# One SBUF room for h2 of all dense tokens from the second merge on, and the dots of two first keys at that merge's end

## Chip, core and metric

The kernel runs on one core of one Trainium2 chip. The metric is the device time of one execution in microseconds. Before the change it is 3731.83 us, the median of three runs (3722.95 to 3736.19).

## What is computed

One decoder block over 1024 tokens of width 1024: an RWKV-7 time mixing and a sparse attention side by side, a merge of both with a layer norm, and PEER, a product-key retrieval of single-neuron experts. The change touches the merge of the second half of the tokens and the beginning of PEER:

```python
merged = sigmoid(z_ga) * y_a + sigmoid(z_gb) * y_b
x  = layer_norm(ALPHA * x + gt1 * (merged @ w_out))
h2 = x * (1 + sc2) + sh2
# _peer(h2): 8 heads, 128 x 128 keys, the best 16 of each half
q = (ht @ w_pq).reshape(T, 8, 2, 64)
s = einsum('thcd,hcnd->thcn', q, sub_keys)
s1, i1 = top_k(s[:, :, 0], 16);  s2, i2 = top_k(s[:, :, 1], 16)
top_s, pos = top_k(s1[..., :, None] + s2[..., None, :], 16)
experts = i1 * 128 + i2 (at pos);  gates = softmax(top_s)
act = gelu(einsum('cd,chkd->chk', h, u_tab[experts])) * gates
out = einsum('chk,chkd->cd', act, v_tab[experts])
```

## The kernel before

Tokens are worked on in two halves H of 512. For each half the program computes both branches, the projection of the attention branch (`merge_b`) and then `merge(H)`. PEER follows. Of its 1024 tokens the first `TD` = 384 (tiles 0 to 2) have their experts' rows gathered from DRAM; the other `DN` = 640 (tiles 3 to 7; a tile has 128 tokens) are done densely: for each of the 128 first keys i1 the dots of all 640 tokens with the 128 experts of that key, times a table of gates that is zero where an expert wasn't chosen, and then the second table.

All float32 products are made of two parts, hi and lo (`whi`, `wlo` for weights): ACT copies the raw weight to `whi`, POOL subtracts it from the raw one to give `wlo`, and PE runs hi by hi, hi by lo and lo by hi. `copy` (L233) is ACT's copy; where a line reads L233, the names on it tell which step it is.

`merge(1)` works in this order: the split of the RWKV output into `ya`; `wbra` (L424 to L426 on PE, sums `zs` L1023 and L1024 on DVE, split into `big`); `wout` (sum `vt` L1043 on DVE); the layer norm with its transposes; h2 with its split into `h2T`; then `wq` in eight heads, whose result goes to the DRAM tensor `qTD`. `ya` and then `h2T` lie in one tile, `Q`, of 128 x 2 x 8 x 512 numbers (hi and lo). After the split, two POOL DMAs store `h2T` to the DRAM tensor `h2TD` (merge 0 stores its 128 dense tokens there too). Beside the merge, a generator `side` retrieves the experts of tiles 1 to 3 on DVE; a step of it (one of four for a tile) is four score tables `sc` (transposing matmuls L1134 on PE from `qT`, a load of `qTD`; copies on ACT), and on DVE four MAX8 (L1143), four MATCH_REPLACE8 (L1145), four MAX8 (L1147) and eight FIND_INDEX8 (L1149, L1151).

Then `retr1` begins. Eight POOL DMAs read `h2TD` back into a new tile `h2T` of 128 x 2 x 8 x 640 (L1633). From it `dots_ahead` takes the dots of 69 first keys, ahead of the dense stage: for one key SP loads `raw` (L1273), ACT makes `whi`, POOL `wlo` (L1277), PE runs 48 matmuls of 128x320 in 24 pairs (L1290, L1292, L1294), ACT copies the result to `ds` and SP stores it to `dotD`. Three keys stand first; after that, in `beside`, steps of the retrieval of tiles 4 to 7 (DVE), batches of the gate tables of tiles 3 to 7, gathers for tiles 0 to 2 (POOL, DVE) and two keys of dots take turns. A tile's gate table can begin when its slots are there (transposes L1239 on PE, waiting for DVE's L1199); a batch of it is 8 copies `gt` and 2 copies `st` on ACT and transposes L1264 on PE. What is left of tables and dots is done at the end of `retr1`. The dense stage follows, in which PE runs the other dots and the second table for all 128 keys.

The order of the instructions on each engine is set by the scheduler of the tile framework, which plays the program through a timeline of its own and puts on each queue what it finds ready first; each engine works through its queue in that order.

Of the kernel before, what the change touches and what calls it, by code (L numbers as in the profile page):

```python
# [8 lines left out]
F32 = mybir.dt.float32  # L9
F32R = mybir.dt.float32r  # L10
# [14 lines left out]
RB = 2  # L25
WB = 3
# [9 lines left out]
REUSE = "tile"  # L36
# [7 lines left out]
QIB = 2  # L44
GM = 1
# [7 lines left out]
DN = 1024 - TD  # L53
# [150 lines left out]
def body(tc, a, out, dbg=None, ntiles=8, mark=lambda s: None):  # L204
# [16 lines left out]
    def prw():  # L221
        return banks[0].tile([128, 512], F32, name="rw", bufs=4)
# [782 lines left out]
    def merge(H, y, bz, mp, side, ties):  # L1005
        t0 = H * 512
        big = lambda name: (bz if name == "big" else mp).tile([128, 2, 8, 512], F32R, name=name)
# [52 lines left out]
        for tt in range(4):  # L1060
            pl = [pacc(), pacc()] if tt == PA else [prw(), prw()]
            for d in range(8):
                nc.tensor.transpose(pl[d // 4][:, d % 4 * 128:(d % 4 + 1) * 128], vt[:, d, tt * 128:tt * 128 + 128], ident)
            xn = mp.tile([128, 1024], F32, name="xn", bufs=4)
            xns.append(xn)
            layernorm(xn, pl, mp)
            for n in range(2):
                pl = ptp()
                for d in range(4):
                    nc.tensor.transpose(pl[:, d * 128:(d + 1) * 128], xn[:, (4 * n + d) * 128:(4 * n + d + 1) * 128], ident)  # L1070
                copy(hl[:, 4 * n:4 * n + 4, tt * 128:tt * 128 + 128], pl.rearrange("p (a b) -> p a b", a=4))
# [9 lines left out]
        if c0 < 512:  # L1081
            for n in range(2):
                G.dma_start(h2TD[:, n, :, dst], h2T[:, n, :, c0:])
# [14 lines left out]
        for h in range(8):  # L1098
# [9 lines left out]
            if H:  # L1108
                next(side, None)

# [371 lines left out]
    h2TD = tc.dram_tile([128, 2, 8, DN], F32R, name="h2TD")  # L1482
# [15 lines left out]
    for H in range(2):  # L1498
# [109 lines left out]
        if H == 1:  # L1608
            tkp = tc.tile_pool(reuse_waits=REUSE, name="tk", bufs=1, side="right")
            tk = tkp.__enter__()  # L1610
        with tc.tile_pool(reuse_waits=REUSE, name=f"mg{H}", bufs=1) as mp:
# [6 lines left out]
            merge(H, ys[4 * H + 3], big, mp, side, ties if H == 0 else iter(()))  # L1618
# [7 lines left out]
    with tc.tile_pool(reuse_waits=REUSE, name="du", bufs=1) as du, \  # L1626
            tc.tile_pool(reuse_waits=REUSE, name="pg", bufs=1, space=PSUM) as pg:

        for name, bufs in (("raw", RB), ("whi", WB), ("wlo", WB)):
            du.tile([128, 1024], F32 if name == "raw" else F32R, name=name, bufs=bufs)  # L1630
        h2T = du.tile([128, 2, 8, DN], F32R, name="h2T")
        for k in range(8):
            G.dma_start(h2T[:, :, k], h2TD[:, :, k])  # L1633
        act = {}
        mark("retr1")
        with tc.tile_pool(reuse_waits=REUSE, name="slots", bufs=1) as sl, \
# [18 lines left out]
            def dots_ahead():  # L1655
                for i1 in ahead:
# [97 lines left out]
```

## Time and profile before

| | |
|---|---|
| median of three runs | 3731.83 us |
| the profiled execution | 3729.43 us |
| its span in the trace | 3727.7 us |
| PE, DVE, ACT, POOL busy | 94%, 69%, 45%, 53% of the span |
| `merge(1)` | about 1488 to 1651 us |
| `retr1` | about 1651 to 2351 us |
| dense stage | about 2351 to 3727 us |

Times within a trace count from the start of the span. PE's busy share is that of pipelined matmuls and says little alone; the stretches below, the waits and the timelines of single engines say which engine sets the pace in a stage. A row of a timeline reads: start, duration, engine, line, operation, what it writes and reads, shape, count, and in brackets how long the engine had been idle and whose end released it. Rows of several instructions alike are put together as x2 and so on.

### The profile page before, as it was taken

The page shows a single profiled execution, that of the slowest core. Times are in us where ns is not written, and L with a number is a line of the kernel's source. Part 1 is how long each engine was busy: PE and PEld are TensorE (multiplying, and loading weights), DVE is VectorE, ACT ScalarE, POOL GpSimd, SP SyncE. Part 2 cuts the span into 40 slices and gives each one's busy share as a digit, 9 for nine tenths or more (in the row PEclk, how much of TensorE's full clock was granted, in tenths as well). Part 3 has the DMA queues.
Part 4 walks back from the last instruction along what each step waited for, and adds up shares of the span by engine and source line. Part 5 has one row for each costly group of instructions (what it writes and reads, how often), then busy time and mean ns, then how long its engine had stood idle before and what let it go on. Part 6 is the DMA issues. An engine that isn't in the chain of part 4 may idle for free.

```text
span 3727.7 us, 64789 instructions
## 1 busy us (share of the span) xinstructions
PE 3499.9 (94%) x24045; PEld 3135.1 (84%) x24045; DVE 2587.5 (69%) x5433; ACT 1694.3 (45%) x3230; POOL 1987.4 (53%) x1572
## 2 busy tenths in 40 slices
PE   8999999889999989879999999999999999999997
PEld 7677777666677767669999999999999999999987
DVE  7856653847467764899989985467667776677654
ACT  3649953244344443447676688422222322222223
POOL 5442222354455554336656542467677676777655
PEclk9999999989999999989999999999999999999999
DMA  7453323864667666478888874889989999898873
GB/s 232 151 159 104 107 87 124 291 194 163 215 206 224 213 213 207 135 230 319 318 327 316 316 284 151 300 320 324 339 317 331 332 330 338 320 332 325 306 263 120
DMA packets 436880, 920.95 MB, mean 247 GB/s; under 512 B 36452, under 2 KB 195508, under 8 KB 433876
## 3 DMA queue, kind: packets, MB, share of 16 engines
q1 hardware_dynamic: 311956, 498.38, 39.8%
q0 software_dynamic: 124608, 418.43, 31.5%
q8 instruction: 189, 3.10, 0.3%
q14 instruction: 127, 1.04, 0.1%
HBM read 791.59 MB, written 125.08 MB: 246 GB/s over the span
## 4 chain that ended last, share of the span: by engine, by line
PE 51%; DVE 15%; DMA 12%; ACT 7%; issue 6%; POOL 6%; SPq 0%; POOLq 0%; ACTq 0%; DVEq 0%
PE pair L1294 8%; PE pair L1292 8%; PE pair L1290 8%; PE acc L424 4%; PE acc L425 4%; PE acc L426 4%; DMA g<-in_u_dram,gidx 4%; DMA g<-in_v_dram,gidx 3%; ACT gt L233 3%; POOL g L1391 2%; DMA raw<-in_ut_dram 2%; POOL wlo L1277 2%; DVE g L1395 2%; PE tp L1264 2%; PE acc L976 1%
## 5 line engine op out<-in xcount | busy, mean ns | idle before, releaser
L1277 POOL TENSOR_TENSOR wlo<-raw,whi 128x1024 fp32r<-128x1024 f32 x264 | 648.7, 2459 | 378.2 <-ACT whi L233 354.5
L414 POOL TENSOR_TENSOR wlo<-wraw,whi 128x512 fp32r<-128x512 f32 x280 | 371.1, 1328 | 550.7 <-ACT whi L233 497.2
L233 ACT ACTIVATE whi<-raw 128x1024 fp32r<-128x1024 f32 x264 | 278.9, 1057 | 649.4 <-PE pair L1292 382.9
L1391 POOL DMA_INDIRECT g<-in_u_dram,gidx x361 | 376.6, 1043 | 293.7 <-DVE g L1395 187.6
L1399 DVE SCALAR_TENSOR_TENSOR pg<-g,dots,pg 128x1024 f32<-128x1024 f32 x317 | 407.0, 1284 | 146.0 <-DMA g<-in_v_dram,gidx 143.0
L1290 PE MATMUL pair<-A,whi 128*128 128x320 f32 (+2 forms) x2048 | 480.5, 311 | 25.4 <-DVE A L1322 19.4
L1290 PE MATMUL pair<-h2T,whi 128*128 128x320 f32 x2048 | 475.6, 312 | 15.0 <-ACT whi L233 15.0
L1292 PE MATMUL pair<-A,whi 128*128 128x320 f32 (+2 forms) x2048 | 479.9, 311 | 3.8 <-DVE A L1322 3.6
L1294 PE MATMUL pair<-A,wlo 128*128 128x320 f32 (+2 forms) x2048 | 478.7, 310 | 0.8 <-POOL wlo L1277 0.8
L1292 PE MATMUL pair<-h2T,whi 128*128 128x320 f32 x2048 | 474.7, 311 | 0.0
L1294 PE MATMUL pair<-h2T,wlo 128*128 128x320 f32 x2048 | 473.1, 311 | 1.6 <-POOL wlo L1277 1.6
L1391 POOL DMA_INDIRECT g<-in_v_dram,gidx x320 | 311.7, 974 | 187.4 <-DVE pg L1399 90.7
L424 PE MATMUL acc<-big,whi 128*128 128x512 f32 x864 | 356.6, 414 | 23.1 <-DVE zs L532 6.5
L1290 PEld LDWEIGHTS pair<-A,whi 128*128 128x128 f32 x2048 | 347.4, 189 | 28.0 <-issue 19.9
L1290 PEld LDWEIGHTS pair<-h2T,whi 128*128 128x128 f32 x2048 | 343.9, 188 | 16.9 <-ACT whi L233 15.4
L426 PE MATMUL acc<-big,wlo 128*128 128x512 f32 x864 | 351.8, 408 | 1.7 <-POOL wlo L414 1.7
L425 PE MATMUL acc<-big,whi 128*128 128x512 f32 x864 | 349.9, 405 | 2.4 <-DVE big L450 2.3
L1292 PEld LDWEIGHTS pair<-A,whi 128*128 128x128 f32 x2048 | 347.4, 189 | 5.1 <-DVE A L1322 5.1
L1395 DVE SCALAR_TENSOR_TENSOR g<-g,pg 128x1024 f32<-128x1024 f32 x233 | 281.3, 1216 | 101.3 <-DMA g<-in_u_dram,gidx 100.2
L1294 PEld LDWEIGHTS pair<-A,wlo 128*128 128x128 f32 x2048 | 347.5, 189 | 1.0 <-POOL wlo L1277 1.0
L1294 PEld LDWEIGHTS pair<-h2T,wlo 128*128 128x128 f32 x2048 | 342.9, 188 | 3.4 <-POOL wlo L1277 2.4
L1292 PEld LDWEIGHTS pair<-h2T,whi 128*128 128x128 f32 x2048 | 344.1, 188 | 0.6
(482 smaller groups left out, 6673.1 us busy)
## 6 DMA issues: line engine op xcount, KB each, us to landing
raw<-in_vt_dram SPq DMA_DIRECT2D x136, 512.0 KB, 4.2
raw<-in_ut_dram SPq DMA_DIRECT2D x128, 512.0 KB, 5.5
gtD<-st SPq DMA_DIRECT2D x20, 2048.0 KB, 9.8
gt<-gtD SPq DMA_DIRECT2D x32, 1280.0 KB, 14.5
wraw<-in_wz_dram SPq DMA_DIRECT2D x152, 256.0 KB, 3.2
dotD<-ds SPq DMA_DIRECT2D x69, 320.0 KB, 5.7
al<-dotD SPq DMA_DIRECT2D x69, 320.0 KB, 6.5
mw<-in_wada_dram SPq DMA_DIRECT2D x32, 512.0 KB, 5.4
```

What stands on the lines that cost most here:

```text
L233: copy = lambda o, i, **k: A.activation(o, i, AF.Copy, **k)
L414: G.tensor_tensor(lo, raw, hi.bitcast(F32), op=OP.subtract)
L424: mm(pt, lhsT=wh[:, ks], rhs=ah[:, k, :], start=k == 0, stop=False)
L425: mm(pt, lhsT=wh[:, ks], rhs=al[:, k, :], start=False, stop=False)
L426: ins = mm(pt, lhsT=wl[:, ks], rhs=ah[:, k, :], start=False, stop=k == nk - 1)
L1277: G.tensor_tensor(lo, raw, hi.bitcast(F32), op=OP.subtract)
L1290: mm(pts[n], lhsT=wh, rhs=ah[:, h], start=k == 0, stop=False)
L1292: mm(pts[n], lhsT=wh, rhs=al[:, h], start=False, stop=False)
L1294: latest[:] = [mm(pts[n], lhsT=wl, rhs=ah[:, h], start=False, stop=last)]
L1391: G.indirect_dma_start(out=u, out_offset=None, in_=a["u" if n < 2 else "v"], in_offset=bass.IndirectOffsetOnAxis(ap=idx[:, k:k + 1], axis=0))
L1395: V.scalar_tensor_tensor(u, u, 1.0, h2, op0=OP.mult, op1=OP.mult, accum_out=dots[:, k:k + 1])
L1399: V.scalar_tensor_tensor(acc, u, dots[:, k:k + 1], acc, op0=OP.mult, op1=OP.add)
```

## The change

- A tile `h2A` (named `h2T`) of 128 x 2 x 8 x 640 numbers is made before the second merge, on the right side of SBUF, and lives until the end. In the second merge `Q` is no tile of its own but the last 512 of the 640 columns of `h2A`. The 128 dense tokens of the first merge, which are all that is still stored to `h2TD`, are loaded into the first 128 columns at the start of the second merge (two POOL DMAs). The two stores of the second merge and the eight loads at the beginning of `retr1` are gone.
- In the second merge `xn` has two buffers, not four.
- At the end of the second merge, behind `wq`, the dots of the first two keys of `ahead` are taken (48 matmuls each, into the PSUM tiles `rw`), with weights that go through the merge's `wraw`, `whi`, `wlo` in halves; ACT copies each result in two pieces to `zs` and itself issues the two stores to `dotD`. `dots_ahead` begins with the third key, so 67 are left to it.
- The pools of `retr1` are laid out in another order (`gt`, `wlo`, `raw`, `whi`).

```diff
--- before.py
+++ after.py
@@ -42,6 +42,7 @@
 SQ = 6
 XOB = 2
 QIB = 2
+DOTS0 = 2
 GM = 1
 FIRST = 3
 XR = 3
@@ -1002,9 +1003,18 @@
         for _ in rest:
             pass
 
-    def merge(H, y, bz, mp, side, ties):
+    def merge(H, y, bz, mp, side, ties, h2A=None):
+
         t0 = H * 512
-        big = lambda name: (bz if name == "big" else mp).tile([128, 2, 8, 512], F32R, name=name)
+
+        def big(name):
+            if name == "Q" and h2A is not None:
+                return h2A[:, :, :, DN - 512:]
+            return (bz if name == "big" else mp).tile([128, 2, 8, 512], F32R, name=name)
+
+        if h2A is not None:
+            for n in range(2):
+                G.dma_start(h2A[:, n, :, 0:DN - 512], h2TD[:, n])
         ya = big("Q")
         for k in range(4):
             st = stg.tile([128, 512], F32, name="xt")
@@ -1061,7 +1071,7 @@
             pl = [pacc(), pacc()] if tt == PA else [prw(), prw()]
             for d in range(8):
                 nc.tensor.transpose(pl[d // 4][:, d % 4 * 128:(d % 4 + 1) * 128], vt[:, d, tt * 128:tt * 128 + 128], ident)
-            xn = mp.tile([128, 1024], F32, name="xn", bufs=4)
+            xn = mp.tile([128, 1024], F32, name="xn", bufs=2 if H else 4)
             xns.append(xn)
             layernorm(xn, pl, mp)
             for n in range(2):
@@ -1078,9 +1088,9 @@
             if "h2" in dbg:
                 nc.sync.dma_start(dbg["h2"][d * 128:(d + 1) * 128, t0:t0 + 512], h2)
             split_act(h2T[:, 0, d, :], h2T[:, 1, d, :], h2)
-        if c0 < 512:
+        if c0 < 512 and not H:
             for n in range(2):
-                G.dma_start(h2TD[:, n, :, dst], h2T[:, n, :, c0:])
+                G.dma_start(h2TD[:, n], h2T[:, n, :, c0:])
         for tt, xn in enumerate(xns[:max(0, NG - 4 * H)]):
 
             i = H * 4 + tt
@@ -1107,6 +1117,19 @@
             nc.sync.dma_start(qTD[H][:, h, :], qt)
             if H:
                 next(side, None)
+        for i1 in list(ahead)[:DOTS0] if H else ():
+
+            w = split_w(a["ut"][i1], 1024)
+            pts = [prw()[:, 0:DN // 2] for n in range(2)]
+            for k in range(8):
+                wh, wl = w[k // 4]
+                ks = slice(k % 4 * 128, k % 4 * 128 + 128)
+                mm6(pts, wh[:, ks], wl[:, ks], h2A[:, 0, k, :], h2A[:, 1, k, :], k, k == 7)
+            for n in range(2):
+                zs = stg.tile([128, 512], F32, name="zs")[:, 0:DN // 2]
+                copy(zs, pts[n])
+                A.dma_start(dotD[ahead[i1]][:, n * (DN // 2):(n + 1) * (DN // 2)], zs)
+            next(side, None)
 
     def layernorm(dst, src, mp):
 
@@ -1479,7 +1502,7 @@
             early_found[i] = f
 
     qTD = [tc.dram_tile([128, 8, 512], F32, name=f"qTD{i}") for i in range(2)]
-    h2TD = tc.dram_tile([128, 2, 8, DN], F32R, name="h2TD")
+    h2TD = tc.dram_tile([128, 2, 8, DN - 512], F32R, name="h2TD")
     gtD = tc.dram_tile([DN // 32, 128, 128, 32], F32, name="gtD")
     ahead = [i1 for i1 in range(128) if i1 % 8 < (J0 + (i1 // 8 % 16 < EXTRA) if i1 >= 8 else JF)]
     ahead = {i1: n for n, i1 in enumerate(ahead)}
@@ -1606,6 +1629,8 @@
             nc.sync.dma_start(dbg["ya"][:, :, H * 512:H * 512 + 512], yaD[H])
             nc.sync.dma_start(dbg["yb"][:, :, H * 512:H * 512 + 512], ybD[H])
         if H == 1:
+            hp = es.enter_context(tc.tile_pool(reuse_waits=REUSE, name="h2", bufs=1, side="right"))
+            h2A = hp.tile([128, 2, 8, DN], F32R, name="h2T")
             tkp = tc.tile_pool(reuse_waits=REUSE, name="tk", bufs=1, side="right")
             tk = tkp.__enter__()
         with tc.tile_pool(reuse_waits=REUSE, name=f"mg{H}", bufs=1) as mp:
@@ -1615,7 +1640,7 @@
 
                 side = retrieve_all(range(1, M1), tk, keep)
             mark(f"merge{H}")
-            merge(H, ys[4 * H + 3], big, mp, side, ties if H == 0 else iter(()))
+            merge(H, ys[4 * H + 3], big, mp, side, *((ties,) if H == 0 else (iter(()), h2A)))
             for _ in side:
                 pass
         bz.close()
@@ -1626,11 +1651,10 @@
     with tc.tile_pool(reuse_waits=REUSE, name="du", bufs=1) as du, \
             tc.tile_pool(reuse_waits=REUSE, name="pg", bufs=1, space=PSUM) as pg:
 
-        for name, bufs in (("raw", RB), ("whi", WB), ("wlo", WB)):
+        du.tile([128, 20, 128], F32, name="gt", bufs=2)
+        for name, bufs in (("wlo", WB), ("raw", RB), ("whi", WB)):
             du.tile([128, 1024], F32 if name == "raw" else F32R, name=name, bufs=bufs)
-        h2T = du.tile([128, 2, 8, DN], F32R, name="h2T")
-        for k in range(8):
-            G.dma_start(h2T[:, :, k], h2TD[:, :, k])
+        h2T = h2A
         act = {}
         mark("retr1")
         with tc.tile_pool(reuse_waits=REUSE, name="slots", bufs=1) as sl, \
@@ -1653,7 +1677,7 @@
 
 
             def dots_ahead():
-                for i1 in ahead:
+                for i1 in list(ahead)[DOTS0:]:
                     ds = sl.tile([128, DN], F32, name="ds", bufs=4)
                     copy(by_half(ds), dots_u(i1, du, h2T, 2))
                     nc.sync.dma_start(dotD[ahead[i1]], ds)
```

Nearly every queue has another order from the second merge on. On DVE, at the end of the second `merge_b` (its last sums are L999 before, L1000 after; `zs` L1023 before and L1033 after are the first sums of the merge; MAX, MATCH_REPLACE and MAX_INDEX are retrieval steps), before:

```order
L999 SCALAR_TENSOR_TENSOR zs<-zs,acc 128x512
L450 TENSOR_TENSOR Q<-xt,Q 128x384 x2
L999 SCALAR_TENSOR_TENSOR zs<-zs,acc 128x512 x2
L1023 SCALAR_TENSOR_TENSOR zs<-zs,acc 128x512
L1143 MAX v_14009<-sc 128x8
L1024 TENSOR_TENSOR zs<-zs,xt 128x512
L1143 MAX v_14009<-sc 128x8 x3
L1145 MATCH_REPLACE s_14022<-v_14009,sc 128x128
L1149 MAX_INDEX i_14010<-v_14009,sc 128x8
```

and after, around the third of the four last sums:

```order
L451 TENSOR_TENSOR h2T<-xt,h2T 128x384
L1170 MAX v_14014<-s_14027 128x8 x3
L1174 MAX_INDEX i_14015<-v_14014,s_14027 128x8 x4
L1000 SCALAR_TENSOR_TENSOR zs<-zs,acc 128x512
L1166 MAX v_14014<-sc 128x8 x4
L1168 MATCH_REPLACE s_14113<-v_14014,sc 128x128
L1172 MAX_INDEX i_14015<-v_14014,sc 128x8
L1168 MATCH_REPLACE s_14113<-v_14014,sc 128x128
```

Of the retrieval's operations none stands before the first sum of the merge before the change; after it about three whole steps do (59 operations): one ahead of the third sum of L1000, one and a half between the third and the fourth, the rest behind that.

On ACT, between the last `wq` weights and the first dots of `retr1` (`gates` waits for DVE; `wx` are copies of the gate tables' and the retrieval's helpers; `raw` is a weight of `dots_ahead`), before:

```order
L233 ACTIVATE whi<-wraw 128x512
L233 ACTIVATE zs<-acc 128x512
L1215 ACTIVATE gates<-gates 128x128
L233 ACTIVATE zs<-acc 128x512
L233 ACTIVATE keys_15751<-iota 128x1024
L233 ACTIVATE wx<-posb 128x1024 x2
L233 ACTIVATE whi<-raw 128x1024 x2
L233 ACTIVATE wx<-posb 128x1024 x3
L233 ACTIVATE whi<-raw 128x1024 x2
```

and after:

```order
L234 ACTIVATE whi<-wraw 128x512
L234 ACTIVATE zs<-rw 128x320 x2
L1131 DMA dotD<-zs 128x320 x2
L1238 ACTIVATE gates<-gates 128x128
L234 ACTIVATE wx<-posb 128x1024
L234 ACTIVATE zs<-rw 128x320 x2
L1131 DMA dotD<-zs 128x320 x2
L234 ACTIVATE whi<-raw 128x1024
L234 ACTIVATE wx<-posb 128x1024
L234 ACTIVATE whi<-raw 128x1024
```

The weights `wraw` of the two new keys stand ahead of `gates`, the copies of the first key's dots too; the first weight of `dots_ahead` stands behind the copies of the second.

On PE, the last table batches of `retr1` (L1264 before, L1287 after), before:

```order
L1264 MATMUL tp<-gt 128x128 x8
L1292 MATMUL pair<-h2T,whi 128x320 x2
L1294 MATMUL pair<-h2T,wlo 128x320 x2
L1290 MATMUL pair<-h2T,whi 128x320 x2
L1292 MATMUL pair<-h2T,whi 128x320 x2
L1294 MATMUL pair<-h2T,wlo 128x320 x2
L1264 MATMUL tp<-gt 128x128 x8
L1290 MATMUL pair<-h2T,whi 128x320 x2
```

and after:

```order
L1287 MATMUL tp<-gt 128x128 x8
L1315 MATMUL pair<-h2T,whi 128x320 x2
L1317 MATMUL pair<-h2T,wlo 128x320 x2
L1313 MATMUL pair<-h2T,whi 128x320 x2
L1315 MATMUL pair<-h2T,whi 128x320 x2
L1317 MATMUL pair<-h2T,wlo 128x320 x2
L1287 MATMUL tp<-gt 128x128 x48
L1313 MATMUL pair<-h2T,whi 128x320 x2
```

Before, dots stand between any two of the last batches; after, the last six batches stand in one piece, with no dots between them, and the dense stage's dots follow.

## Rows read from the trace of the kernel before

**Rows 1.** Page, fourth part: the chain that ended last
```profile
PE 51%; DVE 15%; DMA 12%; ACT 7%; issue 6%; POOL 6%; SPq 0%; POOLq 0%; ACTq 0%; DVEq 0%
```

**Rows 2.** Windows: us, PE PEld DVE ACT POOL busy, clock, DMA, GB/s
```profile
1465.00:1490.00 25.00, 25.00 (x103) 19.36 (x102) 7.94 (x13) 8.04 (x16) 10.82 (x9) 0.94 0.61 205
1490.00:1541.00 51.00, 39.84 (x171) 29.39 (x169) 50.44 (x261) 18.58 (x35) 14.64 (x12) 0.93 0.47 146
...
1651.00:1666.00 15.00, 0.18 (x1) 0.18 (x2) 13.97 (x56) 4.91 (x7) 2.10 (x4) 0.66 1.13 392
1666.00:1690.00 24.00, 23.74 (x148) 22.91 (x149) 20.72 (x20) 7.70 (x9) 19.59 (x14) 0.93 0.76 256
1690.00:2260.00 570.00, 548.59 (x3912) 533.84 (x3913) 523.94 (x1250) 401.73 (x820) 321.73 (x221) 1.00 0.85 307
2260.00:2300.00 40.00, 39.19 (x288) 38.93 (x288) 18.67 (x21) 33.02 (x71) 11.04 (x5) 1.00 0.41 153
2300.00:2352.00 52.00, 52.00 (x400) 52.00 (x399) 16.45 (x18) 51.38 (x112) 14.90 (x6) 1.00 0.42 163
2352.00:2400.00 48.00, 48.00 (x328) 47.87 (x328) 16.11 (x23) 15.82 (x20) 20.49 (x15) 1.00 0.97 341
```

**Rows 3.** PE's waits in 1465 to 1600: total us, times, longest
```profile
PE acc L424 <- DVE zs L1023: 6.0, 3, 3.5
...
PE acc L424 <- DVE vt L1043: 3.2, 1, 3.2
PE acc L425 <- DVE big L450: 2.1, 1, 2.1
```

**Rows 4.** Timeline, DVE, last sums of merge_b, first sum of the merge
```profile
1479.98 0.69 DVE L999 SCALAR_TENSOR_TENSOR zs<-zs,acc 128x512 f32<-128x512 f32 x1 [3.43 <-PE acc L426]
1486.16 0.69 DVE L999 SCALAR_TENSOR_TENSOR zs<-zs,acc 128x512 f32<-128x512 f32 x1 [5.50 <-PE acc L426]
1488.96 0.69 DVE L1023 SCALAR_TENSOR_TENSOR zs<-zs,acc 128x512 f32<-128x512 f32 x1 [2.11 <-PE acc L426]
```

**Rows 5.** Timeline, DVE: one retrieval step of the second merge
```profile
1491.24 0.67 DVE L1143 MAX8 v<-sc 128x8 f32<-128x128 f32 x3
...
1493.92 0.80 DVE L450 TENSOR_TENSOR big<-zs,big 128x512 fp32r<-128x512 f32 x1
```

**Rows 6.** Timeline, PE, ACT, SP, POOL between wq and the first dots
```profile
1665.82 0.90 PE L1290 MATMUL pair<-h2T,whi 128*128 128x320 f32 x2 [14.96 <-ACT whi L233]
...
1656.23 0.31 ACT L1215 ACTIVATE gates<-gates 128x128 f32<-128x128 f32 x1 [10.31 <-DVE gates L1214]
...
1664.71 2.22 ACT L233 ACTIVATE whi<-raw 128x1024 fp32r<-128x1024 f32 x2 [3.79 <-DMA raw<-in_ut_dram]
...
1657.54 0.84 SPq L1273 DMA_DIRECT2D raw<-in_ut_dram  x2
...
1650.16 2.79 POOL L1633 DMA_DIRECT2D h2T<-h2TD  x4 [0.58 <-issue]
```

**Rows 7.** Timeline, PE: pairs of matmuls of one dots key
```profile
1670.10 0.46 PE L1290 MATMUL pair<-h2T,whi 128*128 128x320 f32 x2
...
1671.28 0.46 PE L1292 MATMUL pair<-h2T,whi 128*128 128x320 f32 x2
```

**Rows 8.** DVE waits in 1594 to 2267; PE at tile 7's slots
```profile
DVE v L1143 <- ACT sc L233: 30.7, 14, 4.9
...
2267.38 0.33 PE L1239 MATMUL tp<-ident,i 128*128 128x128 f32 x1 [0.81 <-DVE i L1199]
```

**Rows 9.** Timeline, ACT and PE in the last table batches
```profile
2317.66 1.12 ACT L233 ACTIVATE whi<-raw 128x1024 fp32r<-128x1024 f32 x1
...
2319.19 1.14 ACT L233 ACTIVATE st<-tp 128x512 f32<-128x512 f32 x2
...
2323.47 1.13 ACT L233 ACTIVATE st<-tp 128x512 f32<-128x512 f32 x2
...
2340.19 1.95 PE L1264 MATMUL tp<-gt 128*128 128x128 f32 x16
```

## The prediction

> **What bounds the kernel now.** I read the chain of waits first. PE carries half of it and DVE 15% [rows 1], so a hole in PE's work is worth looking for, but the chain doesn't tell which engine would be late next if the hole were filled. For that I read the windows by stage, then the waits and timelines at each stage's end.
>
> In the second merge PE has little to wait for except DVE: in 1490 to 1541 DVE is busy for 50.44 of 51 us, while PE works 39.84 [rows 2]; what PE waits for on DVE there is 6.0 + 3.2 + 2.1 = 11.3 us [rows 3]. Just ahead of it, in the last sums of `merge_b`, DVE stands idle: 3.43 + 5.50 + 2.11 = 11.0 us before three sums in a row [rows 4].
>
> Between the last `wq` matmul and the first dots PE stands for 14.96 us [rows 6]. `gates` on ACT waits 10.31 us for DVE, everything behind it in ACT's queue stands too, SP issues the first `raw` at 1657.54, and `whi` begins at 1664.71 [rows 6].
>
> In `retr1` both PE (548.59 of 570 us) and DVE (523.94) are near full [rows 2]. What ends the stage is a chain: DVE finishes the retrieval of tile 7, PE's slots transpose waits for it at 2267.38 [rows 8], and only then can the 16 table batches of that tile follow, which run on ACT: 51.38 of 52 us in 2300 to 2352 [rows 2]. PE is full there as well (52.00), because dots stand between the batches. The dense stage then begins, and PE is full in it (48.00 of 48) [rows 2]. So the end of the kernel moves as the end of `retr1` moves.
>
> **The change part by part.** The sum is made against the profiled execution, 3729.4 us; the median of the runs is 3731.8, so I add 2.4 us for the time that I name.
>
> *The two keys in the hole.* A pair of matmuls takes (1671.28 - 1670.10) / 4 = 0.295 us [rows 7], a key of 24 pairs 7.1 us, two 14.2 us: as long as the hole. Their weights stand ahead of `gates` on ACT, and nothing of them waits for DVE. What stays of the hole is the turn from the second key to the third: two copies and two DMA issues on ACT, then `whi`, which I put at 3 us from ACT's work on one key, 1.53 us for `whi` and `ds` [rows 9], taken twice. So PE gets 12 us ahead at 1666. But this isn't the end of a stage: DVE, 13.97 of 15 us busy in that stretch [rows 2], does not stand in the hole. I count 0 of the 12 us in the sum; the bounds are 0 and -12.
>
> *Where it comes back.* After the change the last six table batches stand on PE with no dots between. A batch takes ACT (2323.47 - 2319.19) = 4.28 us, and PE 1.95 us at most [rows 9]. PE waits 6 x 2.3 = 14 us there: the work that was put into the hole is missing here.
>
> *ACT's work behind tile 7's slots.* The order of before has 16 batches and 8 keys' `whi` and `ds` there, that of after 16 batches and 6 keys': 16 x 4.28 + 8 x 1.53 = 80.7 us against 77.7. That is 3 us off the path, as ACT is what is full; bounds 0 and -3.
>
> *The retrieval moved into DVE's idle time.* Three MAX8, four MATCH_REPLACE8 and four FIND_INDEX8 take 1493.92 - 1491.24 = 2.68 us [rows 5]; a step has five MAX8 (at about 0.2 us) and four FIND_INDEX8 (half of the 2.1 us that the eight others take) more, some 4.7 us. After the change about three steps, 14 us, stand ahead of the merge's first sum. The idle time there is 11.0 us [rows 4]. So 3 us may delay that sum, and 14 us are gone from the stretch in which PE waits 11.3 us for DVE. The retrieval stands at the same operation in both orders when h2 is split, and the work from there to its end is equal, so what the merge gains, DVE keeps to tile 7's slots. I take -8 (11.3 less 3); bounds 0 and -11.3.
>
> *The DMAs.* Two stores and eight loads of `h2T` go. The loads share the hole with the first `raw`, at 392 GB/s and a DMA share of 1.13 [rows 2]; in the hole they cost PE nothing that the dots there don't already give back. The two loads that are new, at the merge's start, take POOL about half of what four took, 2.79 us [rows 6], so 1.4 us, where POOL is busy for 10.82 of 25 us [rows 2]; they are needed only by the dots 150 us later. Without that cover a `wlo` would be 1.4 us late. The third and fourth `xn` buffers aren't missed: PE's transposes of the layer norm stand in the same order as before.
>
> *The clock.* PE's granted clock, a mean of its two levels 1.2 and 2.4 GHz, is 0.66 of full in the hole and 0.93 in the 24 us after it [rows 2], and the first eight pairs take 1670.10 - 1665.82 = 4.28 us in place of 2.36 [rows 6, 7]. So 1.9 us come back at 1666, for PE alone. The six batches with PE idle for more than half of each may cost the same 1.9 us at the first dense dots: bounds 0 and +2; I take 0, since in the stretches of 1490 to 1541, where PE stands a fifth of the time, the clock is still 0.93 [rows 2]. (The Trainium skill, "TensorE: Matmul & The Clock Gate", section "HAM oscillation — how this bites in real kernels", describes bursts of matmuls with idle time between them falling back to the lower clock; by that the +2 would hold, and the sum would be -9.)
>
> Sum: -8 - 3 + 0 = -11 us, with ends of -14 and +2. By the median: 3731.8 - 11 = 3720.8, 3718 to 3734.
>
> **The rivals.**
> A: the hole counts after all. DVE waits 30.7 us in `retr1` for score tables `sc` [rows 8], which come through PE and ACT; with PE 12 us ahead these may come sooner, and then DVE's retrieval ends up to 12 us earlier. For it: 14 such waits, and PE waits only 0.81 us at tile 7's slots [rows 8], so the two engines run nearly level. Against: ACT, not PE, released DVE each time, and the order keeps PE's score transposes among the dots. It gives -8 - 12 = -20: 3712, and 3708 with all of the 11.3. (By the Trainium skill, "Perfetto Trace Analysis", section "Identifying the Most-Contended Engine", weight loads rather than matmul time tell how full PE is, and the fullest engine is the one to relieve; the windows give 533.84 of 570 us for the loads and 523.94 for DVE, which speaks for A, by a little.)
>
> B: nothing arrives. The merge's relief is lost again in the layer norm, where ACT, DVE and PE wait for each other in turn, or `retr1`'s new order loses it in other waits. Then at most ACT's 3 us are left: 3729 to 3732.
>
> C: slower. DVE's queue holds the three retrieval steps ahead of the last sums of `merge_b` and the first of the merge. If their score tables land late, DVE stands, the sums stand behind it, PE's accumulators aren't free, and the whole merge moves. It costs the 14 us of the steps in place of hiding them: -3 + 14 = +11, 3743. It begins to cost when the first score tables come later than 1475, and costs all when they come at 1486.16, at the fourth sum [rows 4]. Against it: in the new order the first four score transposes stand 12 matmuls earlier on PE, and ACT has 8 of 25 us to do there [rows 2].
>
> That the dots don't land in the hole, since `gates` stands ahead of them on ACT, would be B as well; the order speaks against it.
>
> **How the numbers follow.** Forecast 0.48, A 0.19, B 0.22, C 0.11. A measurement can tell about 0.3% here, 11.2 us. The forecast lies on that edge, so half of it (0.24) is faster and half the same; A is faster; B is the same; of C 0.01 is the same. Faster 0.24 + 0.19 = 0.43, same 0.24 + 0.22 + 0.01 = 0.47, slower 0.10. The likeliest gives 3721. The range goes from A with all of the merge's relief, 3708, up into the middle of C, between 3732 and 3743: 3738. Some 0.16 is left out, most of it C's upper and A's lower end.
>
> **What would show it.** Right: PE stands about 3 us where it stood 14.96; DVE's retrieval runs before 1489, and PE's waits for `zs`, `vt` and `big` in the merge fall from 11.3 us to about 3; tile 7's slots come near 2259; PE stands some 14 us in all in the last six batches while ACT is full; dense starts near 2340. A is right if tile 7's slots come near 2247 and DVE's waits for `sc` are down by some 12 us. B is right if they come at 2265 or later though the hole is filled. C is right if DVE waits for `sc` ahead of the sums L1000. All of it falls if `retr1` ends on something else than ACT's batches, such as a dots key or a gather.

## The result, and the profile after

The changed kernel is slower: 3749.93 us against 3736.40, the medians of ten runs each, a ratio of 1.0051 with a 95% interval of 1.0035 to 1.0066. A second comparison, beside other kernels, gave 1.0029 (1.0012 to 1.0047). The forecast was 3721 us, and 3738 the upper end of its range, counted from 3731.83 us for the kernel before, which has 3736.40 here; the ratio does not depend on that.

The two profiled executions of the changed kernel took 3765.97 us (span 3764.2) and 3759.29 (span 3757.5), each the longest of its ten runs, so I compare stretches, not spans. All stretches below count from one mark, the start of the last operation of L808 on `yall` on DVE (L809 after; at 1464.4 us before, 1465.6 after). Up to it DVE and PE have the same order in both kernels. "Split" is the end of the last of the eight DVE operations that make h2 (L1077 before, L1087 after), beside which it is split into hi and lo; a tile's slots are the start of its first slots transpose on PE.

The windows of the changed kernel, with the columns of [rows 2] (us, then busy time of PE, PEld, DVE, ACT and POOL with counts, granted clock, DMA share, GB/s); the last three go from tile 5's slots to tile 6's, from these to tile 7's, and from these to the end of the last table batch:

```profile
1465.00:1490.00 25.00, 25.00 (x118) 18.93 (x117) 19.28 (x81) 7.56 (x16) 9.90 (x9) 1.00 0.83 226
1490.00:1541.00 51.00, 37.24 (x155) 27.68 (x154) 48.43 (x235) 16.83 (x31) 16.43 (x12) 0.93 0.55 161
1541.00:1600.00 59.00, 52.00 (x235) 41.27 (x234) 31.21 (x61) 34.69 (x59) 18.09 (x15) 0.90 0.35 111
1651.00:1666.00 15.00, 14.35 (x97) 14.08 (x96) 14.08 (x89) 3.78 (x8) 2.58 (x2) 1.00 0.53 180
1666.00:1690.00 24.00, 12.94 (x63) 12.28 (x64) 21.87 (x50) 8.73 (x11) 14.91 (x11) 0.72 0.51 180
...
1995.30:2153.90 158.60, 151.15 (x1058) 147.10 (x1058) 144.94 (x334) 107.35 (x211) 89.19 (x61) 0.99 0.86 311
2153.90:2285.30 131.40, 128.73 (x927) 125.74 (x927) 106.09 (x309) 98.17 (x202) 55.68 (x35) 1.00 0.64 240
2285.30:2366.00 80.70, 70.08 (x513) 68.76 (x514) 31.38 (x32) 78.04 (x173) 15.41 (x7) 0.96 0.41 151
```

The retrieval did move into DVE's idle time: DVE works 19.28 of 25 us in 1465 to 1490, where it worked 7.94 [rows 2]. The hole is filled: PE is busy for 14.35 of the 15 us in which it did 0.18. But the next stretch gives most of that back: 12.94 of 24 us against 23.74, at a clock of 0.72 against 0.93. And the end of `retr1` is later: counted from the mark the last table batch ends at 900.4 us, in place of 886.9.

Where PE stands now between the merge and `retr1` (timelines of PE and ACT of the changed kernel):

```profile
1672.22 0.90 PE L1313 MATMUL pair<-h2T,whi 128*128 128x320 f32 x2 [6.86 <-ACT whi L234]
...
1677.70 0.90 PE L1313 MATMUL pair<-h2T,whi 128*128 128x320 f32 x2 [4.05 <-ACT whi L234]
...
1668.64 0.31 ACT L1238 ACTIVATE gates<-gates 128x128 f32<-128x128 f32 x1 [9.63 <-DVE gates L1237]
...
1675.64 1.06 ACT L234 ACTIVATE wx<-posb 128x1024 bf16<-128x1024 bf16 x1 [3.48 <-DVE posb L1233]
1676.61 1.04 ACT L234 ACTIVATE whi<-raw 128x1024 fp32r<-128x1024 f32 x1
```

`gates` stands on ACT between the copies of the first and the second key, and it can begin only at 1668.6, 203.1 us after the mark, where it was 191.9 before [rows 6]. The copies of the second key, and the weight of the third behind them, wait for that: PE's 6.86 us. Its 4.05 us are for the next weight, which stands on ACT behind a copy `wx` that waits 3.48 us for DVE.

The same places, kernel before and after, in us:

| | before | after | after, second profile |
|---|---|---|---|
| mark to the split of h2 | 129.9 | 130.6 | 130.2 |
| split to tile 3's slots | 95.1 | 105.8 | 106.5 |
| tile 3's slots to tile 4's | 148.5 | 144.3 | 144.8 |
| tile 4's to tile 5's | 149.1 | 149.1 | 148.3 |
| tile 5's to tile 6's | 148.5 | 158.6 | 157.1 |
| tile 6's to tile 7's | 131.9 | 131.4 | 132.0 |
| tile 7's slots to the last table's end | 83.9 | 80.6 | 80.6 |
| last table's end to the end of the span | 1376.4 | 1398.2 | 1396.2 |

Down to the last table all of it repeats within 1.5 us: 13 us are lost there, all of them on the way to tile 7's slots. The last line does not explain the result. Among the profiles of this study that have no dots left over there, it lies between 1375 and 1398 us, and 13 us there and 20 more here would make a ratio of 1.009, which neither comparison found (the upper ends of their intervals are 1.0066 and 1.0047).

### The profile page after: what moved, and what is told of

Its sections match the earlier page's. It is cut to its first block, busy times and chain, and to the rows that moved or that the text cites. A ratio compares the mean times of both kernels' runs of the same rounds, so it can differ in the third digit from the quotient of the medians.

```text
span 3764.2 us, 64785 instructions
## 1 busy us (share of the span) xinstructions
PE 3522.9 (94%) x24045; PEld 3153.4 (84%) x24045; DVE 2589.6 (69%) x5433; ACT 1697.2 (45%) x3235; POOL 1979.8 (53%) x1566
## 5 line engine op out<-in xcount | busy, mean ns | idle before, releaser
L1300 POOL TENSOR_TENSOR wlo<-raw,whi 128x1024 fp32r<-128x1024 f32 x262 | 636.8, 2432 | 407.4 <-ACT whi L234 384.3
L1313 PE MATMUL pair<-A,whi 128*128 128x320 f32 (+2 forms) x2048 | 483.8, 313 | 34.7 <-DVE A L1345 29.9
L1313 PE MATMUL pair<-h2T,whi 128*128 128x320 f32 x2016 | 469.0, 312 | 11.7 <-ACT whi L234 10.9
L1315 PE MATMUL pair<-h2T,whi 128*128 128x320 f32 x2016 | 469.0, 312 | 0.0
L1313 PEld LDWEIGHTS pair<-h2T,whi 128*128 128x128 f32 x2016 | 338.9, 189 | 13.6 <-ACT whi L234 11.6
L1315 PEld LDWEIGHTS pair<-h2T,whi 128*128 128x128 f32 x2016 | 339.8, 189 | 1.0
```

The lines of the kernel that those rows point to most:

```text
L1300: G.tensor_tensor(lo, raw, hi.bitcast(F32), op=OP.subtract)
L1313: mm(pts[n], lhsT=wh, rhs=ah[:, h], start=k == 0, stop=False)
L1315: mm(pts[n], lhsT=wh, rhs=al[:, h], start=False, stop=False)
```

## The experiments

Three theories stood at the start. The first: the dots in the hole do the harm, through what ACT, POOL and DVE do beside them. The second: the harm is done in the merge, where the retrieval now stands ahead of the last sums of `merge_b`. The third: DVE's retrieval sets the end of `retr1`, and each build's order of `retr1` decides how long DVE idles there.

One table for all kernels but one, by the profile of each. Its "end of `retr1`" is the later of the last table's end and the start of the last copy `ds` of ahead-taken dots, both counted from the mark, against the kernel before; what is later is set in bold.

| kernel | split to tile 7's slots | last table | last `ds` | end of `retr1` | ratio (95% interval) |
|---|---|---|---|---|---|
| before | 673.1 | **886.9** | 885.9 | 0 | |
| changed | 689.1 | **900.4** | 880.0 | +13.5 | 1.0051 (1.0035 to 1.0066) |
| changed, again | 688.6 | **899.4** | 878.9 | +12.5 | 1.0029 (1.0012 to 1.0047) |
| a: no keys in the hole | 694.1 | **902.8** | 865.4 | +15.9 | 1.0064 (1.0039 to 1.0089) |
| b: one key in the hole | 682.5 | **894.0** | 864.0 | +7.1 | 1.0032 (1.0017 to 1.0048) |
| c: before, two keys left out | 670.0 | **881.2** | 861.7 | -5.7 | 0.9989 (0.9974 to 1.0005) |
| d: changed, `FIRST` 1 | 689.0 | **901.6** | 880.4 | +14.7 | 1.0054 (1.0035 to 1.0074) |
| e: changed, retrieval pinned | 675.2 | **888.5** | 868.0 | +1.6 | 0.9987 (0.9970 to 1.0004) |
| f: before, scores one step ahead | 666.6 | 881.3 | **900.1** | +13.2 | 1.0041 (1.0022 to 1.0060) |
| g: changed, scores one step ahead | 662.0 | 881.0 | **887.3** | +0.4 | 0.9995 (0.9977 to 1.0012) |
| h: g without keys in the hole | 655.9 | 874.4 | **891.6** | +4.7 | 0.9996 (0.9974 to 1.0019) |
| i: g with four keys in the hole | 677.1 | **891.1** | 879.3 | +4.2 | 0.9994 (0.9976 to 1.0012) |
| j: g with the retrieval pinned | 662.7 | 879.0 | **885.4** | -1.5 | 0.9993 (0.9980 to 1.0006) |

The end of `retr1` explains the measured ratios: the kernels that lie 7 to 16 us behind measure 1.003 to 1.006, those within 6 us of before measure 0.999 to 1.000 with intervals that hold 1. So the place where the time is lost is the stretch that ends with `retr1`, and the question is why that end moved.

**a and b. Fewer keys in the hole.**

The edit of a; b has 1 in place of 0:

```diff
-DOTS0 = 2
+DOTS0 = 0
```

> The changed kernel with h2A kept, but no dots at the merge's end (69 keys left to dots_ahead). Theory 1 (the dots in the hole do the harm, through what ACT, POOL and DVE do beside them): the harm is gone, ratio to before 0.997 to 1.001, tile 3's slots near 1690, hole of PE 10 to 15 us. Theory 2 (the harm comes with the new order of the merge, where the retrieval stands ahead of the last sums of merge_b, and has nothing to do with the dots): ratio 1.003 to 1.006, last sum of merge_b near 1491 and tile 3's slots near 1700. Theory 3 (DVE sets the end of retr1, and each build's own order of retr1 decides how long DVE idles there): DVE's idle time from the split of h2 to tile 7's slots, 47 us before and about 62 after, and the end of retr1 move together, whichever way.

> The changed kernel with the dots of one key at the merge's end, not two. Theory 1: half the harm, ratio about 1.0025. Theory 2: the whole harm, 1.005. Theory 3: no rule between the number of keys and the time; the end of retr1 follows DVE's idle time.

Without any dots at the merge's end the harm is the largest of all (+15.9 us, 1.0064), with one key the smallest (+7.1, 1.0032). Theory 1 falls: the dots in the hole don't do it. What both share with the changed kernel is the new room of h2 and the retrieval that runs ahead in the merge: 59 of its operations stand ahead of the merge's first sum in all three, none in the kernel before. The split of h2 comes 130.3 to 130.5 us after the mark, as in the changed kernel and within 0.6 us of before, so the loss isn't in the merge itself. (The idle times of DVE in the expectation of a, 47 and 62 us, are 51.8 and 64.3 by the windows shown under e.)

**c. Fourteen us of PE's work less in the kernel before.** The two keys' dots are left out (the third key's result is stored in their places).

```diff
-                for i1 in ahead:
+                for i1 in list(ahead)[2:]:
...
+                    if ahead[i1] == 2:
+                        for n in range(2):
+                            nc.sync.dma_start(dotD[n], ds)
```

> The kernel before, with the dots of the first two keys left out (their places in dotD take the third key's dots): 14 us of PE's work in retr1 is gone. If PE's work in retr1 counts for the end (rival A of the prediction), ratio 0.9965 or less, 13 us. If DVE's retrieval and then ACT's table batches set the end (theory 3), 0.999 to 1.001, with 3 us less of ACT's work behind tile 7's slots and PE idle between the last batches; larger moves either way would come from the order alone and show in DVE's idle time.

The end of `retr1` comes 5.7 us sooner, not 14, and the time is the same within the interval (0.9989). Most of PE's spare time isn't worth anything here: the last `ds` comes 24 us sooner, and the last table only 5.7. The forecast had put the worth of the hole between 0 and 12 us and counted 0; this build measures it directly, though its queues have a new order too.

**d. Three keys ahead of tile 3's slots, not five.**

```diff
-FIRST = 3
+FIRST = 1
```

> The changed kernel with FIRST at 1 in place of 3: with the two keys at the merge's end, three keys in all stand ahead of tile 3's slots, as before, and not five. If the keys ahead of the slots on PE hold tile 3 up, its slots come from 1702 back to about 1690 and the ratio falls to about 1.001. If DVE holds them up (theory 3), they stay at 1700 or later and the ratio stays near 1.005, unless the new order gives DVE other idle time.

Tile 3's slots come 4.9 us sooner after the split (100.9), and tile 7's don't (689.0). What the first stretch wins is lost in the next, 150.8 us against 144.3. The keys ahead of the slots aren't it.

**e. The retrieval back behind the merge's first sum.** The steps called in the `wbra` loop are queued on DVE behind the first sum of the merge; everything else of the program is as changed, with both keys in the hole.

```diff
-            if H == 0 or d % 2:
+            if H and d % 2:
+                with tc.issue_after(anchors[2][0].ins):
+                    next(side, None)
+            elif H == 0:
                 next(side, None)
```

> The changed kernel, with the retrieval steps that are called from the wbra loop queued on DVE behind the merge's first sum, as they stood before the change. If the retrieval moved ahead of the sums of merge_b does the harm (theory 2, rival C of the prediction), the split of h2 and tile 3's slots come back to before's places (130 us after the last yall sum, 95 us after the split) and the ratio is about 1.000. If it doesn't, tile 3's slots stay at 100 us or more after the split and the ratio at 1.003 to 1.006.

The time is that of before again: 0.9987, and tile 7's slots are at 675.2 us, not 689.1. The last build below has the same pin and has them at 675.4, while the four builds without it and without another cure lie between 682.5 and 694.1. So the harm comes with the retrieval that was moved ahead. But it doesn't come the way that theory 2 had it: tile 3's slots stay at 104.0, and the split is 2.5 us later than in the changed kernel. The loss lies from tile 5's slots to tile 6's. The windows of the pinned kernel, tile 5's slots to tile 6's and tile 6's to tile 7's:

```profile
1994.80:2139.80 145.00, 143.00 (x1021) 139.48 (x1021) 133.23 (x331) 104.70 (x209) 85.39 (x57) 1.00 0.89 325
2139.80:2272.70 132.90, 129.16 (x926) 125.45 (x925) 107.55 (x309) 98.26 (x202) 54.35 (x35) 1.00 0.64 237
```

Beside the changed kernel's (above) the first is 13.6 us shorter, with 11.7 us less of DVE's time. Some of that is three gather sums fewer (42 against 45, at 1.25 us); they only stand earlier, since both kernels have 147 of them between the split and tile 6's slots (142 before). More is the same instructions taking less time: some operations of DVE that meet a subtraction of POOL last until it ends (shown in the last section). The second window is 131 to 133 us in both. It is 128 to 135 us in every kernel of the table, with 13 to 40 gather sums in it, so sums that stand ahead of tile 6's slots cost their time there and save none behind.

The whole way from the split to tile 7's slots, of the kernel before, the changed one, e and g:

```profile
1594.30:2267.40 673.10, 633.03 (x4330) 603.90 (x4328) 621.27 (x1662) 443.46 (x884) 369.05 (x259) 0.98 0.83 298
...
1596.20:2285.30 689.10, 657.06 (x4456) 628.54 (x4454) 624.84 (x1663) 448.76 (x892) 368.87 (x253) 0.98 0.77 280
...
1597.50:2272.70 675.20, 650.48 (x4459) 622.85 (x4458) 615.74 (x1662) 447.96 (x893) 366.01 (x253) 0.99 0.79 286
...
1608.20:2270.20 662.00, 633.16 (x4280) 602.34 (x4279) 612.60 (x1631) 443.45 (x884) 369.74 (x250) 0.98 0.80 288
```

DVE is busy for 621.3, 624.8 and 615.7 us in the first three, with the same instructions, and idle for 51.8, 64.3 and 59.5. So the pin brings the kernel back to the time of before by another way than the harm came: of its 14 us, 9 are DVE's operations taking less time, and 5 are idle time. The idle time of e is still 8 us above that of before.

**f and g. The score tables one step ahead.** In the changed kernel DVE stands idle for 64.3 us between the split and tile 7's slots, against 51.8 before. Two of the largest of these waits, by who released DVE:

```profile
DVE v L1166 <- ACT sc L234: 38.0, 15, 5.9
...
DVE gt L1278 <- issue: 6.8, 3, 4.8
```

The first was 30.7 us [rows 8]. The longest of them, timelines of PE, ACT and DVE of the changed kernel:

```profile
2219.14 1.15 PE L1157 MATMUL tp<-keysT,qT 64*128 64x128 f32 x8
...
2219.43 3.40 ACT L234 ACTIVATE gt<-gt,slots 128x128 f32<-128x128 bf16 x8
2222.71 1.07 ACT L234 ACTIVATE whi<-raw 128x1024 fp32r<-128x1024 f32 x1
2223.66 0.70 ACT L234 ACTIVATE ds<-pair 128x640 f32<-128x640 f32 x1
2224.25 0.65 ACT L234 ACTIVATE sc<-tp 128x256 f32<-128x256 f32 x2
...
2224.66 0.87 DVE L1166 MAX8 v<-sc 128x8 f32<-128x128 f32 x4 [5.88 <-ACT sc L234]
```

PE has made the scores at 2220.3, and ACT first does a table batch, a weight and a dots copy, in the order of its queue, before it copies them for DVE, which has stood since 2218.8. In f and g the matmuls and copies of a step's scores are written one step ahead, before the DVE operations of the step before it:

```diff
-        for h2_ in range(4):
+        def scores(h2_):
             qT = tp_.tile([128, 2, 128], F32, name="qT", bufs=2)
...
             sc = tp_.tile([128, 4, 128], F32, name="sc", bufs=2)
             for e in range(2):
                 copy(sc[:, e:4:2, :], pts[e][:, 0:2, :])
+            return sc
+
+        ready = scores(0)
+        for h2_ in range(4):
+            sc = ready
+            if h2_ < 3:
+                ready = scores(h2_ + 1)
```

> The changed kernel with the score tables of a retrieval step written ahead of the step before it (matmuls and copies of sc one step earlier, the two sc buffers as they were). If DVE's waits for sc (38 us from the split of h2 to tile 7's slots, of 65 idle) set the end of retr1 (theory 3), they fall to some 15 us, tile 7's slots come 15 to 20 us sooner after the split, and the ratio to the kernel before is 0.998 to 1.001. If something else holds DVE or the end of retr1, the waits move elsewhere and the ratio stays at 1.004 to 1.006.

> The kernel before with the score tables written one step ahead. Theory 3: DVE's waits for sc fall from 31 us to some 12, and the end of retr1 comes about 12 to 15 us sooner: ratio about 0.996. If the waits for sc don't set the end, ratio 0.999 to 1.002.

In the changed kernel (g) it did what theory 3 said: the wait is halved, tile 7's slots come 27 us sooner, and the ratio is 0.9995. Only 15 of the 27 us are idle time, though. 12 are busy time (612.6 against 624.8): one retrieval step more, 32 instructions, is done by the split, and fewer operations meet POOL's. The wait that is left, of kernel g:

```profile
DVE v L1173 <- ACT sc L234: 18.6, 11, 3.4
```

In the kernel before (f) DVE's part is better too (666.6), the last table ends 5.6 us sooner, and yet the kernel is slower, 1.0041. There PE has become what is last: some 120 matmuls of ahead-taken dots stand behind the last table batch, where the kernel before has none, and the last `ds` comes at 900.1. Of the 20 us that follow the last table in f, PE is busy for 18.51 and ACT for 5.55:

```profile
2350.00:2370.00 20.00, 18.51 (x127) 18.25 (x126) 0.00 (x0) 5.55 (x7) 5.72 (x3) 1.00 0.95 336
```

My expectation for f was wrong because it looked at DVE alone. Between f and g PE's hole counts: PE stands there for 16.4 us in f and for 5.1 in g, and g's last `ds` is 12.8 us ahead of f's.

**h, i and j. More of both.**

On top of the edit of g, h has `DOTS0` at 0 and i has it at 4; j has the edit of e. The edit of i:

```diff
-DOTS0 = 2
+DOTS0 = 4
```

> The changed kernel with the score tables one step ahead and no dots at the merge's end. With the score tables ahead, dots are left over behind the last table batch, so PE should be what ends retr1. If that is so, the dots in the hole are worth their 14 us now: ratio about 1.003 to 1.004, against 0.9995 with two keys in the hole. If DVE or ACT still ends the stage, 0.999 to 1.001.

> The changed kernel with the score tables one step ahead and four keys at the merge's end. If PE ends retr1 there, and the 7 and 4 us that PE still stands behind the two keys are filled too, another 5 to 10 us: ratio 0.997 to 0.998. If DVE's chain ends it again, or ACT stands at gates either way, 0.999 to 1.001.

> The changed kernel with both cures: the retrieval queued behind the merge's first sum, and the score tables one step ahead. If the two add up, the end of retr1 comes 10 us sooner than with the score tables alone, ratio 0.997. If either alone brings DVE's chain down to where PE ends the stage, no more than 0.999.

h missed: without the keys in the hole its last `ds` is 4.3 us behind g's, not 14, and its time is the same (0.9996). The hole itself is only 6.4 us long there; PE stands for 11.7 us between the split and tile 3's slots, and for 7.9 in g. i missed as well: PE is no longer last, and tile 7's slots are back at 677. j has the earliest end of `retr1` of the changed kernels (-1.5 us) and measures 0.9993 (0.9980 to 1.0006). With the score tables ahead (g and j) `retr1` is at a point where the table batches and PE's dots end within some 6 us of each other, and the pin adds little: tile 7's slots are at 662.7 us with it and at 662.0 without. So in these builds the moved retrieval does harm only together with the late score tables. No kernel of this study is measurably faster than the one before.

**The changed kernel again, and the drain at the end.**

> The changed kernel again, for a second profile. If what the first profile shows of retr1 is the kernel's own, the stretch from the split of h2 to tile 7's slots is 689 us again, within 3 us, and the dense stage, 1398 us in the first profile against 1376 before, is the part that differs, as it holds most of the 16 us by which that execution lay above the median.

> The kernel with the retrieval queued behind the merge's first sum, and the POOL transfers of h2 cut into as many pieces as the kernel before issues (12 in place of 4, the same bytes). All builds with the new h2 room stand 20.6 us from PE's last matmul to the end of the span, the kernel before 14.8; what is longer is POOL's last drain. If that goes by the number of POOL's transfers, it is 14.8 us here; if not, 20.6.

The first gave the third column of the table above: `retr1` repeats, 688.6 against 689.1. The dense stage does not differ as expected, 1396.2 us again, while the other kernels with the new room and no dots left over have 1375 to 1391. PE waits 26 to 30 us for DVE's `A` there, 19 before. Whether part of that belongs to the changed order stays open; the medians leave little room for it. The second divides the POOL transfers of h2 (12 in place of 4, the pinned kernel otherwise; it isn't in the table, since that moves the mark from which the table counts: the split comes 123.3 us after it, and 133.1 in e):

```diff
             for n in range(2):
-                G.dma_start(h2A[:, n, :, 0:DN - 512], h2TD[:, n])
+                for k in range(0, 8, 2):
+                    G.dma_start(h2A[:, n, k:k + 2, 0:DN - 512], h2TD[:, n, k:k + 2])
...
-                G.dma_start(h2TD[:, n], h2T[:, n, :, c0:])
+                for k in range(0, 8, 4):
+                    G.dma_start(h2TD[:, n, k:k + 4], h2T[:, n, k:k + 4, c0:])
```

The end stayed 21.0 us from PE's last matmul, and the ratio was 1.0006 (0.9990 to 1.0023). The number of transfers isn't what makes POOL's last drain longer.

## Why the prediction was wrong

**The hole and the dots: placed as read, of no use, and less is saved than I said.** Two keys did take its place. I put what is left of it at 3 us; it is 6.86 + 4.05 us, because I took the weights as free of DVE and overlooked that the *copies* of the second key stand behind `gates` on ACT, and a later weight behind `wx`, both of which wait for DVE. PE ahead or not had been given 0 in the sum, with rival A beside it. Kernel c answers it: 14 us of PE's work less are worth 5.7 us at the end of `retr1`, and no measurable time.

**ACT's work behind tile 7's slots: right.** Put at -3, measured -3.3 (83.9 to 80.6). PE stands in the last batches for 10.6 us, where I said 14. The clock term, 0 out of 0 to +2, was right too: the clock is at 0.96 in the last batches, and the first eight pairs of dots behind them take 2.43 us, where 2.36 is the full-speed time of the forecast. The waits of PE in 2285 to 2366 of the changed kernel:

```profile
PE tp L1287 <- ACT st L234: 10.6, 6, 3.8
```

**The merge's relief: the term that was sized wrong.** Put at -8, measured +0.7 (129.9 to 130.6 us to the split). The 11.3 us for which PE waits for DVE [rows 3] were read as time that the merge would gain. They became 7.7 + 6.0 + 1.1 = 14.8 us; PE stands idle for 20.8 us in 1465 to 1600, where it was 18.6. And DVE's idle time has only moved: 17.6 us before the `vt` sums, where it was 6.5. PE's waits for DVE in 1465 to 1600 of the changed kernel, the windows of the kernel before and the changed one, and DVE's waits before `vt` in the same two:

```profile
PE acc L425 <- DVE zs L1033: 7.7, 6, 2.2
PE acc L425 <- DVE posb L1206: 6.0, 1, 6.0
...
PE acc L425 <- DVE vt L1053: 1.1, 1, 1.1
```

```profile
1465.00:1600.00 135.00, 116.40 (x514) 90.54 (x513) 101.70 (x386) 61.03 (x109) 42.77 (x33) 0.94 0.45 143
...
1465.00:1600.00 135.00, 114.24 (x505) 87.88 (x504) 98.93 (x375) 59.08 (x105) 44.42 (x34) 0.93 0.51 151
```

```profile
DVE vt L1043 <- PE acc L426: 6.5, 3, 5.0
...
DVE vt L1053 <- PE acc L427: 17.6, 4, 5.1
```

What DVE had done sooner it put in front of the first sums. Counted from the mark, the last sum of `merge_b` comes at 25.3 us (21.8 before), the first of the merge at 30.0 (24.6). Timeline of DVE in the changed kernel:

```profile
1490.86 0.66 DVE L1000 SCALAR_TENSOR_TENSOR zs<-zs,acc 128x512 f32<-128x512 f32 x1
...
1493.49 0.49 DVE L1166 MAX8 v<-sc 128x8 f32<-128x128 f32 x2 [1.43 <-ACT sc L234]
...
1495.58 0.67 DVE L1033 SCALAR_TENSOR_TENSOR zs<-zs,acc 128x512 f32<-128x512 f32 x1
```

That is the delay of that sum for which the forecast allowed 3 us, at 5.4. Rival C's mechanism, late score tables, has 1.4 us of it, and the merge makes all but 0.7 us up by the split.

**"What the merge gains, DVE keeps to tile 7's slots": the step that failed.** I counted DVE's work from the split to tile 7's slots, found it equal in both orders, and took its idle time as given. The instructions were the same and took 621.3 and 624.8 us; the idle time went from 51.8 to 64.3. Both together are +16 us on a stretch for which I had +0. With the merge's +0.7 and ACT's -3.3 that is, but for rounding, the 13.5 us by which `retr1` ends later, where the sum had -11. The order of a queue decides not only how much stands ahead of an instruction but also whether what it waits for is there, and all queues had been put in a new order. Kernel e shows which part of the change set that off: the retrieval ahead in the merge; with it pinned, tile 7's slots come 2.1 us later than before and not 16, though the idle time itself falls by 5 us only. Kernel g shows that the score tables one step ahead are another way to undo the harm, 15 us of idle time among the 27 that they bring.

What is not shown is why the scheduler's order of `retr1` is worse after the retrieval has moved: the end of `retr1` lies 7 to 16 us later in four builds with the moved retrieval (the changed kernel, a, b, d) without following the number of keys, and I have no rule that would have told the size from the program. Every build here, e and g too, has all its queues in an order of its own, and none holds DVE's queue to the order of before with the rest of the change in place.

**The rivals.** A was given 0.19 and fell with c. B, that nothing arrives, named `retr1`'s new order as a cause, and its sign came (tile 7's slots later than 2265 though the hole is filled: 2285); but it stopped at no change. C had the right direction and 0.11, by a mechanism that hardly appeared: no wait for `sc` stands ahead of the last sums of `merge_b`, and 1.4 us ahead of the merge's first. That a new order of a stage that is nearly full on PE and DVE can lose 13 us had no place among them, and the range, up to 3738, ended before it.

## What to carry to other kernels

In a stage like this one, where PE and DVE are both over 90% busy [rows 2], equal work on the pacing engine's queue doesn't mean equal time: its idle time is a second term, it has to be forecast too, and a scheduler's new order of all queues may move it by more than the edit is worth. Before filling a hole on an engine, leave the same amount of its work out (kernel c): if the end moves by much less, most of the hole is worth nothing. And when a change lets the scheduler start something sooner, pin it where it was and measure once more (kernel e): that tells whether the harm hangs on the early start, but not by which waits, since the pinned build has a new order as well.

## What the runs showed that I had not expected

- Some operations of DVE are held up by POOL. The 36 operations L1197 (128x1024 in bf16, two inputs) between the split and tile 7's slots took 36.0 us before, 37.9 in the changed kernel and 34.7 in e, single ones 0.66 to 2.79 us. Over the 14 profiles there are 504 of them: the 333 that met no subtraction of POOL (`wlo`) took 0.66 to 0.75 us, and the 121 that took longer than 0.76 all met one, and every one of them ended 0.54 to 0.56 us after such a subtraction did. One of them, POOL and DVE of the changed kernel:

```profile
2274.67 2.73 POOL L1300 TENSOR_TENSOR wlo<-raw,whi 128x1024 fp32r<-128x1024 f32 x1 [6.05 <-ACT whi L234]
...
2275.16 2.78 DVE L1220 TENSOR_TENSOR wp<-ge,df 128x1024 bf16<-128x1024 bf16 x1
```

  The gather sums (128x1024 in f32, two inputs) don't show it: 163 of them began beside such a subtraction in the kernel before and took 1.20 to 1.29 us. Over the stretch the same instructions took 616 to 629 us in the kernels that have all of them there. By an estimate from these traces nearly all of that difference is such waits: taking off what an operation took over the usual time of its kind leaves 568 to 570 us in each of these kernels, and 47 to 60 us of waiting.
- After PE's last matmul the kernel before needs 15.1 us to the end of the span and every kernel with the new room 20.9, with the same operations; what is longer is POOL's last drain, 5.2 us before and 11.2 after. It isn't the number of POOL's transfers. The ratios of e, g and j leave it no room either, so it may be the profiled execution's own; that is not shown.
- From the start to the mark, up to which PE and DVE have the same order in all kernels of the table, profiled executions differ by 19 us (1455.2 to 1474.4). A difference of 13 us is seen in stretches from a common mark, and in medians of ten runs, but not in two spans.
